# A three-MoE network: the branch for overfull experts moved behind the sixth pair, small loads issued in the mixers

## The chip, the cores and the metric

The kernel runs on one core of a Trainium2 chip. The metric is the device time of one execution in microseconds (us), lower is better. A core has five engines that run their own instruction streams and meet through semaphores: TensorE (PE: matmuls; its weight loads are shown as PEld), VectorE (DVE), ScalarE (ACT), GpSimd (POOL) and SyncE (SP, which here only issues DMAs). 16 DMA engines carry all transfers between the chip's memory (HBM) and the on-chip memory. "PEq", "SPq" and so on are the engines' sequencers: branches, register loads, semaphore instructions, DMA issues.

## The reference

x has T = 256 tokens of D = 1024. Three layers follow each other, each a mixer and a mixture of experts (MoE): first the "even" mixer, then the "odd" mixer, then a "second" mixer of another kind, and a norm at the end. Cut to the MoE, of which all three are alike:

```python
g_logits = xt @ w_group + b_group;  g_sel = argmax(g_logits)            # 4 groups
p_g = softmax(g_logits)[g_sel]
e_in = (xt @ w_expert + b_expert).reshape(N, 4, 8)[:, g_sel]            # 8 experts of the group
top_v, top_i = lax.top_k(e_in, 2)                                       # 2 experts for each token
gate = p_g * softmax(top_v)
y_e = (silu(xr @ w1[e]) * (xr @ w3[e])) @ w2[e]                         # for the rows xr of expert e, hidden size 512
out = segment_sum(y * gate)                                             # back to the tokens
x = x + gate2 * out                                                     # gate2 in the first two layers only
```

All is float32. The weights of the 32 experts of one MoE are 192 MB (w1, w3, w2 of 2 MB each, times 32), and every one of them is read once. The inputs are fixed, so that the number of tokens of each expert is, too; no expert has over 64 tokens in any of the three MoEs.

## The kernel before

**Tiles.** The tokens lie in two tiles of 128. An expert has room for CAP = 64 tokens, and two experts make a pair, so a MoE is a loop over NP = 16 pairs. For pair p: `up(p, "g")` and `up(p, "u")` multiply the pair's gathered tokens `xg` with w1 and w3 (32 matmuls each), `turn(p)` transposes the product `hh` on PE into `ht`, `down(p)` multiplies with w2. `parts`, at the end of `down`, takes the product out of PSUM: DVE multiplies with `ga` into `sg`, ACT rounds into `yh`, POOL puts the rest into `yl`. `combine(p, t)` scatters yh and yl back to token tile t by matmuls with the one-hot `pg`, and DVE adds to `x`. `gather(j)` collects the tokens of pairs 2j and 2j + 1 into `xg` from the high and low parts `hh`, `hl` of the normed tokens. The loop delays the combine: `combine(p - 1, 0)` stands between the two ups of pair p, `combine(p - 1, 1)` behind its turn. `gather(p // 2 + 1)` stands between up "u" and the turn of each odd pair p.

**Weights.** All large weights go through a ring of RING = 18 slots of 1 MB. A list (`plan`) fixes the order of the loads; `pump` (its DMA is line 193) issues the next of them on SP whenever a slot is free, at the place of the program where `done` or `release` frees one. A pair needs 12 loads. In a MoE two slots hold `hh` and `hl`, and one holds `hT`, the transposed tokens; hT's slot is released behind the branch.

**DMA lanes.** The DMAs of SP and ACT share eight completion semaphores ("lanes", DMAHW0 to DMAHW7 in the rows of the order below) in the program's order. A DMA is issued only when the one that is eight places ahead of it has landed.

**Small loads.** `router(l)` issues four DMAs on ACT (the router's weights `wr` and biases `br` of MoE l), `bias_load` one of 1 MB (`bias` from `bvec`, in rows of 1 KB) for the odd mixer, `second_setup` eleven (constants of the second mixer: k_rope, k_rot, k_vmask and others). All stand in pair 0: MoE0's `start` issues bias_load(1) and router(1), MoE1's router(2) and second_setup, and MoE2 loads the final norm's weights (512 KB) there.

**The branch.** `overflow` reads the largest rank (`ti`) into a register of every engine (line 1716) and branches on it (line 1717): where an expert has over 64 tokens, a loop over all experts recomputes what did not fit. With the inputs of this kernel that body never runs, and each engine jumps over it. The branch stands behind gather(0), ahead of pair 0. Behind it SP waits for the lanes that the body uses, all eight.

The order of work in the mixers comes from `weave`, which interleaves generators by estimated times; instructions are issued in the order in which the program records them. In the odd mixer `gate_coeffs(1, 2)` ends with two copies on ACT into `ga`; ACT's next work is a CAST (line 460) that splits weights and three copies into `pT` for the attention's matmuls.

Of the kernel before, what the change touches and what calls it, by code (L numbers as in the profile page):

```python
# [9 lines left out]
FT = mybir.dt.float32  # L10
# [3 lines left out]
AF = mybir.ActivationFunctionType  # L14
OP = mybir.AluOpType
# [10 lines left out]
NEG = -1e30  # L26
E = 32
CAP = 64
RING = 18
SLOT = 2048  # L30
SCRATCH = 2048
# [90 lines left out]
class Net:  # L122
# [746 lines left out]
    def even(self, coeffs):  # L869
        nc = self.nc  # L870
        with self.tc.tile_pool(name="even", bufs=1, reuse_waits="tile") as g:
# [49 lines left out]
            def stream():  # L921
                yield from self.slab_tm(512, s_qa)

                def use_att():
                    s = self.slot()
                    self.att, self.ob = s[:, :1024], s[:, 1024:]
                    self.flag("att", 0.7)

                def use_vb():
                    s = self.slot()  # L930
                    self.vb, self.gs = (s[:, 1024 * i:1024 * i + 1024].rearrange("p (t d) -> p t d", t=NT) for i in range(2))

                yield from self.mix(self.slab_tm(256, s_ka), 8, self.ev[0])
                self.want(use_att)
                self.want(use_vb)
                yield from self.mix(self.slab_fm(4, s_qb), 16, self.ev[1])
                self.outputs(4)
                self.outputs(4)
                self.gate_coeffs(0, 2)
                yield (1.8, 5.0)  # L940
                self.router(0)
                yield from self.mix(self.slab_tm(512, s_vb), 8, self.ev[2])
                yield from self.mix(self.slab_tm(512, s_rb), 8, self.ev[3])
                self.release(2)
# [33 lines left out]
    def odd(self, coeffs):  # L978
        nc, A, tc = self.nc, self.A, self.tc
        with tc.tile_pool(name="odd", bufs=1, reuse_waits="tile") as g:  # L980
# [77 lines left out]
            def stream():  # L1058
# [3 lines left out]
                self.outputs(8)  # L1062
                yield from self.mix(self.slab_tm(512, s_v(4)), 8, self.od[1])
                self.gate_coeffs(1, 2)
                yield (3.8, 0.3)
                yield from self.mix(self.slab_tm(512, s_qk(3)), 8, self.od[2])
                yield from self.mix(self.slab_tm(512, s_qk(1)), 8, self.od[3])
# [369 lines left out]
    def second(self, coeffs):  # L1437
        nc, tc = self.nc, self.tc
        with tc.tile_pool(name="sec", bufs=1, reuse_waits="tile") as g:
# [98 lines left out]
            def stream():  # L1538
# [3 lines left out]
                yield from t(h, KC, [[(f, 0, P, s_kraw(1)), (0, P, 152, s_vv(1, 0)), (1, P, 152, s_vv(1, 1))]])  # L1542
                self.outputs(4)
                self.outputs(4)
                yield from self.slab_fm(4, s_q)
                yield from self.slab_fm(4, s_f)
                yield from self.slab_fm(4, s_hq)
# [162 lines left out]
        for i in range(n):  # L1710
            self.mm(p[:, :476], self.ident, self.km, True, True)

    def overflow(self, g, l, hT, h, rk, wt, ti, w1, w3, w2, gate):
        nc, tc = self.nc, self.tc
        wd = self.dp.tile([E, P, NT], FT, name="wd", tag="wd")
        rv = nc.values_load(ti, min_val=0, max_val=T, skip_runtime_bounds_check_because="rank < T")
        with tc.If(rv >= CAP):
            wv = g.tile([P, NT, E], FT, name="wv")
            nc.vector.tensor_scalar(wv, rk, float(CAP), None, op0=OP.is_ge)
            nc.vector.tensor_mul(wv, wv, wt)  # L1720
            nc.scalar.dma_start(wd.rearrange("e p t -> p t e"), wv, allow_slow_non_contiguous=True)
            if gate:
                self.gate_coeffs(l, 5)
            for t in range(NT):
                for k0 in (0, 4):
                    p = self.psum().rearrange("d (k q) -> d k q", k=4)
# [4 lines left out]
                        self.affine(hT[:, k0 + k, P * t:P * t + P], p[:, k], k0 + k, "v")  # L1731
            with tc.For_i(0, E, 1) as e:
                wc = g.tile([P, NT], FT, name="wc")
                nc.scalar.dma_start(wc, wd[bass.ds(e, 1)].rearrange("e p t -> (e p) t"))
                ho = g.tile([P, 4, T], FT, name="ho", tag="yh")
                chunk = lambda tag: g.tile([P, 512], FT, name=tag)
                for hc in range(4):
                    pp = [self.psum((P, T)), self.psum((P, T))]
                    for j in range(2):
                        c0 = P * hc + 64 * j  # L1740
                        for p, w, tag in zip(pp, (w1, w3), ("hh", "ht")):
                            c = chunk(tag).rearrange("p (k n) -> p k n", k=KC)
                            nc.scalar.dma_start(c, w[bass.ds(e, 1)].rearrange("e (p k) n -> (e p) k n", k=KC)
                                                [:, :, c0:c0 + 64])
                            for k in range(KC):
                                self.mm(p[64 * j:64 * j + 64], c[:, k], hT[:, k], k == 0, k == KC - 1)
                    nc.scalar.activation(ho[:, hc], pp[0], AF.Silu)
                    nc.vector.tensor_mul(ho[:, hc], ho[:, hc], pp[1])
                for nq in range(8):
                    c = chunk(("hh", "ht")[nq % 2]).rearrange("p (k n) -> p k n", k=4)  # L1750
                    nc.scalar.dma_start(c, w2[bass.ds(e, 1)].rearrange("e (k p) n -> (e p) k n", p=P)
                                        [:, :, P * nq:P * nq + P])
                    for t in range(NT):
                        p = self.psum((P, P))
                        for hc in range(4):
                            self.mm(p, ho[:, hc, P * t:P * t + P], c[:, hc], hc == 0, hc == 3)
                        tmp = g.tile([P, 512], FT, name="sg", bufs=2)
                        nc.vector.tensor_scalar(tmp[:, :P], p, wc[:, t:t + 1], None, op0=OP.mult)
                        if gate:
                            nc.vector.tensor_mul(tmp[:, :P], tmp[:, :P], self.ga[:, P * nq:P * nq + P])  # L1760
                        xs = self.x[:, t, P * nq:P * nq + P]
                        nc.vector.tensor_add(xs, xs, tmp[:, :P])

    def moe(self, l, mods, start, coeffs, slots, fill=None):
        nc, tc = self.nc, self.tc
        _, w1, w3, w2, gate = self.moe_args(l)
        with tc.tile_pool(name="moe", bufs=1, reuse_waits="tile") as g:
            hT = self.hT
# [157 lines left out]
            gather(0)  # L1926
            if late is not None:
                late()
            self.pump()
            self.overflow(g, l, hT, (hh, hl), rk, wt, ti, w1, w3, w2, gate)  # L1930
            self.release()
            weighted(0)
            for p in range(NP):
                last = p == NP - 1
# [11 lines left out]
                    turn(p)  # L1946
                else:
                    up(p, "g")
                    if p:
                        combine(p - 1, 0)  # L1950
                    else:
                        gather_w(0)
                        start()
                        if l == 2:
                            nc.scalar.dma_start(fw, self.A["final_norm_2"].rearrange("(o n) -> o n", o=1)
                                                .to_broadcast([P, D]))
                    up(p, "u")
                    if p % 2:
                        gather(p // 2 + 1)
                        if p == NP - 3:  # L1960
                            self.release(2, reserve=min(2, slots))
                    gather_w(p + 1)
                    turn(p)
                    if p:
                        combine(p - 1, 1)
                if fill is not None:
                    fill(p)
                (down_last if last else down)(p)
                if p == NP - 2:
                    coeffs()  # L1970
            if l == 2:
# [26 lines left out]
def body(tc, A, out):  # L1998
    with ExitStack() as ctx:
# [7 lines left out]
        n.plan_moe(2)  # L2007

        n.reserve = 6
        n.even(lambda: n.norm_coeffs(0, 7, 3, 4))  # L2010
# [9 lines left out]
        n.moe(0, n.ev[6], start0, lambda: n.norm_coeffs(1, 6, 0, 1), 8,  # L2020
              lambda p: 4 <= p < 8 and n.bias_flip(n.bias1, n.bias1, p - 4))
        n.odd(lambda: n.norm_coeffs(1, 7, 3, 4))
        bp.close()
        n.rb.close()
        pb = ctx.enter_context(ExitStack())
        pre = pb.enter_context(tc.tile_pool(name="pre", bufs=1))
# [6 lines left out]
        n.moe(1, n.od[5], start1, lambda: n.norm_coeffs(1, 8), 14)  # L2033
        n.fb.close()
        n.second(lambda: n.norm_coeffs(1, 9))
        pb.close()
# [29 lines left out]
```

## Time and profile before

| | |
|---|---|
| median of 3 runs | 2110.97 us (2109.19 to 2112.38) |
| the profiled execution | 2108.36 us |
| its span, first to last instruction | 2106.3 us |
| PE busy | 1901.6 us, 90% of the span |
| DVE, ACT, POOL busy | 858.1, 427.5, 327.9 us |
| moved by the DMA engines | 725.35 MB, 344 GB/s over the span |
| mean granted clock of TensorE | 0.968 |

MoE0's first up starts at 231.4 us, MoE1's at 879.4 and MoE2's at 1645.9; MoE0's pairs end at about 705, MoE1's at about 1340, and MoE2 runs to the end. The span is what the trace covers; the 2 us around it belong to the time. "Granted clock" is the share of TensorE's full 2.4 GHz; its lower level is 0.5 (1.2 GHz). An idle of an engine is put down to what released it; "issue" means that the profile shows no releaser.

### The profile page before, as it was taken

How to read it: one execution, taken by the hardware profiler on the slowest of the kernel's cores; microseconds unless marked ns; L12 is line 12 of the kernel's file. 1: busy time of each engine (PE TensorE's matmuls, PEld its weight loads, DVE VectorE, ACT ScalarE, POOL GpSimd, SP SyncE). 2: the span in 40 equal slices, each digit the busy share in tenths (PEclk: the TensorE clock that was granted, in tenths of full speed). 3: DMA queues.
4: the chain of work that ended last, by engine and by line, in shares of the span. 5: the costliest groups of instructions: out<-in, count | busy, mean ns of one | idle time of the engine just before them, and what ended most of it. 6: DMA issues, size and time to landing. Idle time of an engine off the chain costs nothing. (4 is left out here: it accounts for less than half of the span.)

```text
span 2106.3 us, 24926 instructions
## 1 busy us (share of the span) xinstructions
PE 1901.6 (90%) x9930; PEld 1056.1 (50%) x9930; DVE 858.1 (41%) x1574; ACT 427.5 (20%) x778; POOL 327.9 (16%) x248
## 2 busy tenths in 40 slices
PE   6888799999999899899999999998899899999997
PEld 3656344444444667534444444586788344444443
DVE  3665333333322567533332232467666333232223
ACT  1423101111100343211110011254544111010011
POOL 1331100000000334100000000142444000000000
PEclk8998899999999999999999999998999999999999
DMA  9697799999999856799999999921357799999997
GB/s 323 238 319 297 260 422 421 422 421 421 421 421 406 300 222 244 294 365 421 421 421 421 421 421 421 326 101 41 125 194 300 292 421 421 421 421 422 421 421 285
DMA packets 157547, 725.35 MB, mean 344 GB/s; under 512 B 25305, under 2 KB 43088, under 8 KB 85226
## 3 DMA queue, kind: packets, MB, share of 16 engines
q1 hardware_dynamic: 139216, 716.84, 84.9%
q10 hardware_dynamic: 18201, 6.76, 1.3%
q8 instruction: 85, 1.39, 0.3%
q14 instruction: 45, 0.36, 0.0%
HBM read 722.48 MB, written 1.07 MB: 344 GB/s over the span
## 5 line engine op out<-in xcount | busy, mean ns | idle before, releaser
L257 PE MATMUL ps<-slot,xg 128*64 128x512 f32 x2992 | 710.5, 599 | 20.6 <-DMA slot<-moe_w 9.6
L257 PEld LDWEIGHTS ps<-slot,xg 128*64 128x64 f32 x2992 | 254.4, 138 | 422.0 <-issue 359.8
L257 PE MATMUL ps<-slot,ht 128*64 128x512 f32 (+1 forms) x1552 | 345.0, 574 | 56.4 <-issue 49.2
L257 PE MATMUL ps<-slot 128*128 128x256 f32 (+8 forms) x2230 | 368.4, 327 | 15.1 <-DVE slot L461 9.6
L257 PEld LDWEIGHTS ps<-slot 128*128 128x128 f32 (+3 forms) x2230 | 300.5, 187 | 73.6 <-issue 14.0
L257 PEld LDWEIGHTS ps<-slot,ht 128*64 128x64 f32 x1552 | 128.7, 139 | 228.4 <-issue 213.9
L1891 DVE TENSOR_TENSOR x<-x,ps 128x512 f32<-128x512 f32 x180 | 115.3, 682 | 277.0 <-PE ps L257 277.0
L1865 POOL TENSOR_TENSOR yl<-sg,yh 128x512 fp32r<-128x512 f32 (+1 forms) x68 | 82.5, 1213 | 884.8 <-ACT yh L1864 884.8
L462 POOL TENSOR_TENSOR slot<-slot 128x512 fp32r<-128x512 f32 (+2 forms) x108 | 164.4, 1539 | 273.2 <-ACT slot L460 261.9
L1844 DVE SCALAR_TENSOR_TENSOR hh<-sg,ws,ps 128x512 f32<-128x512 f32 x48 | 53.4, 1113 | 319.4 <-PE ps L257 179.8
L1864 ACT CAST yh<-sg 128x512 fp32r<-128x512 f32 (+1 forms) x68 | 40.3, 593 | 468.9 <-DVE sg L1863 468.9
L461 DVE TENSOR_TENSOR slot<-slot 128x512 fp32r<-128x512 f32 (+2 forms) x108 | 110.2, 1035 | 54.4 <-ACT slot L460 53.9
L1863 DVE TENSOR_TENSOR sg<-ps,ga 128x512 f32<-128x512 f32 (+1 forms) x68 | 44.9, 660 | 175.2 <-PE ps L257 175.2
L460 ACT CAST slot<-slot 128x1024 fp32r<-128x1024 f32 (+2 forms) x108 | 106.6, 1020 | 46.2 <-PE ps L257 27.3
L257 PEld LDWEIGHTS ps<-u,slot 128*128 128x128 f32 x768 | 96.9, 199 | 18.3 <-issue 17.0
L257 PE MATMUL ps<-u,slot 128*128 128x256 f32 x768 | 101.9, 293 | 0.0
L1840 ACT ACTIVATE sg<-ps 128x512 f32<-128x512 f32 x48 | 28.7, 598 | 312.4 <-PE ps L257 312.4
L257 PE MATMUL ps<-yh,pg 128*128 128x512 f32 (+1 forms) x204 | 87.1, 429 | 0.7 <-ACT yh L1864 0.7
L257 PE MATMUL ps<-yl,pg 128*128 128x512 f32 (+1 forms) x204 | 77.5, 382 | 0.9 <-POOL yl L1865 0.8
L1916 POOL TENSOR_TENSOR slot<-x,rows 128x512 f32<-128x512 f32 x2 | 2.5, 1272 | 464.5 <-DVE x L1912 464.5
L398 ACT ACTIVATE xg<-ps,cf 128x256 f32<-128x256 f32 x64 | 36.2, 565 | 156.6 <-PE ps L257 156.6
L1867 ACT CAST yh<-ps 128x512 fp32r<-128x512 f32 (+1 forms) x34 | 19.1, 561 | 227.3 <-PE ps L257 227.2
(334 smaller groups left out, 1586.4 us busy)
## 6 DMA issues: line engine op xcount, KB each, us to landing
slot<-moe_w SPq DMA_DIRECT2D x376, 1024.0 KB, 19.8
slot<-w_gate SPq DMA_DIRECT2D x59, 1024.0 KB, 17.7
slot<-w_up SPq DMA_DIRECT2D x59, 1024.0 KB, 19.8
slot<-w_down SPq DMA_DIRECT2D x50, 1024.0 KB, 18.1
slot<-ada_w SPq DMA_DIRECT2D x48, 1024.0 KB, 7.7
slot<-w_in SPq DMA_DIRECT2D x20, 1024.0 KB, 8.5
slot<-odd_w_in SPq DMA_DIRECT2D x12, 1024.0 KB, 13.1
more<-w_down SPq DMA_DIRECT2D x10, 1024.0 KB, 19.8
```

What stands on the lines that cost most here:

```text
L257: self.nc.tensor.matmul(out, lhsT=lhsT, rhs=rhs, start=start, stop=stop)
L398: self.nc.scalar.activation(out, p, AF.Identity, scale=a, bias=nb[:, k:k + 1])
L460: nc.scalar.copy(wh, src)
L461: nc.vector.tensor_sub(wl[:, 0], src[:, 0], wh[:, 0].bitcast(FT))
L462: nc.gpsimd.tensor_sub(wl[:, 1], src[:, 1], wh[:, 1].bitcast(FT))
L1840: nc.scalar.activation(sg, ps, AF.Silu)
L1844: nc.vector.scalar_tensor_tensor(ha.rearrange("s k p -> s p k"), st["sg", p].rearrange("s (p k) -> s p k", k=4), st["ws", p], ps.rearrange ...
L1863: nc.vector.tensor_mul(y, ps, self.ga[:, sl])
L1864: nc.scalar.copy(yh, y)
L1865: nc.gpsimd.tensor_sub(yl, y, yh.bitcast(FT))
L1867: nc.scalar.copy(yh, ps)
L1891: nc.vector.tensor_add(self.x[:, t, sl], self.x[:, t, sl], ps)
```

## The change

Four things are moved. (1) The branch stands behind `down` of pair LATE = 5, the sixth; ahead of it both combines of pair 5, behind it gather(3), which were a pair later and ahead of pair 5's turn. (2) The body is written anew, with three DMAs in a loop inside a loop, so that its DMAs use three lanes. (3) hT's slot is released as soon as the router's logits are there. (4) The small loads are issued in the mixers ahead: bias_load(1) in the even mixer, router(1) and second_setup in the odd one, router(2) and the final norm's weights in the second.

```diff
@@ even mixer
                 self.router(0)
+                self.bias_load(1, self.bias1)
@@ odd mixer
                 self.gate_coeffs(1, 2)
+                self.router(1)
+                self.second_setup(self.pre)
                 yield (3.8, 0.3)
@@ second mixer
                 self.outputs(4)
+                self.router(2)
...
                 coeffs()
+                nc.scalar.dma_start(self.rows[1], self.A["final_norm_2"].rearrange("(o n) -> o n", o=1).to_broadcast([P, D]))
@@ overflow
             with tc.For_i(0, E, 1) as e:
...
+                with tc.For_i(0, 4, 1) as c:
                     pp = [self.psum((P, T)), self.psum((P, T))]
+                    for p, w, tag in zip(pp, (w1, w3), ("yh", "yl")):
+                        wt_ = g.tile([P, KC, P], FT, name="w" + tag, tag=tag)
+                        nc.scalar.dma_start(wt_, w[bass.ds(e, 1)].rearrange("e (p k) n -> (e p) k n", k=KC)
+                                            [:, :, bass.ds(c * P, P)])
...
+                    wt_ = g.tile([P, D], FT, name="wd", tag="yh")
+                    nc.scalar.dma_start(wt_, w2[bass.ds(e, 1)].rearrange("e h n -> (e h) n")[bass.ds(c * P, P)])
@@ moe
             self.route_logits(1)
+            self.release()
...
-            self.pump()
-            self.overflow(g, l, hT, (hh, hl), rk, wt, ti, w1, w3, w2, gate)
-            self.release()
             weighted(0)
...
                     up(p, "g")
-                    if p:
+                    if p and p - 1 != LATE:
                         combine(p - 1, 0)
-                    else:
+                    elif not p:
                         gather_w(0)
                         start()
-                        if l == 2:
-                            nc.scalar.dma_start(fw, self.A["final_norm_2"].rearrange("(o n) -> o n", o=1)
-                                                .to_broadcast([P, D]))
                     up(p, "u")
-                    if p % 2:
+                    if p % 2 and p != LATE:
                         gather(p // 2 + 1)
...
                     turn(p)
-                    if p:
+                    if p and p - 1 != LATE:
                         combine(p - 1, 1)
...
                 (down_last if last else down)(p)
+                if p == LATE:
+                    combine(p, 0)
+                    combine(p, 1)
+                    self.overflow(g, l, (hh, hl), rk, wt, ti, w1, w3, w2, gate)
+                    gather(p // 2 + 1)
@@ body
-        def start0():
-            n.bias_load(1, n.bias1)
-            n.gate_coeffs(0, 5)
-            n.router(1)
...
-        def start1():
-            n.gate_coeffs(1, 5)
-            n.router(2)
-            n.second_setup(pre)
```

In the rows of the order below a row with x2 or more stands for so many alike; line numbers of helpers are higher by one in the changed kernel (L193 is L194, L257 is L258), those of the branch by five. The order on SP, MoE0, where the branch stood: the last load of the first ring, the rank's load into a register, the branch and its first inner jump, which names the lanes.

```order
L193 DMA slot<-moe_w 128x2048 [waits DMAHW0_49,PE_49]
L1716 TENSOR_LOAD ti [waits DVE_49]
L1717 COMPARE_AND_BRANCH
L1732 COMPARE_AND_BRANCH
L1732 UNCONDITIONAL_BRANCH [waits DMAHW0_49,DMAHW1_49,DMAHW2_49,DMAHW3_49,DMAHW4_49,DMAHW5_49,DMAHW6_49,DMAHW7_49]
```

And where it stands in the changed kernel, 73 rows further on, behind the loads that pairs 0 to 5 release.

```order
L194 DMA slot<-moe_w 128x2048 [waits DMAHW2_49,PE_49]
L1721 TENSOR_LOAD ti [waits DVE_49]
L1722 COMPARE_AND_BRANCH
L1737 COMPARE_AND_BRANCH
L1737 UNCONDITIONAL_BRANCH [waits DMAHW3_49,DMAHW4_49,DMAHW5_49]
```

SP's branch moved past the loads of six pairs, and the lanes that it names are three, the oldest ones, where there were eight.

The order on PE, MoE0, around the branch, first in the kernel before: the end of gather(0), the branch, the first rows of the body (the body has 234 rows of matmuls in all, counting repeats).

```order
L257 MATMUL ps<-u,slot 128x256 [waits PE_49]
L257 MATMUL ps<-u,slot 128x256 x7
L1716 TENSOR_LOAD ti [waits DVE_49]
L1717 COMPARE_AND_BRANCH
L257 MATMUL ps<-rows_121,sel 128x512 [waits DVE_49,PE_49]
L257 MATMUL ps<-rows_121,sel 128x512
```

Then in the changed kernel: the end of pair 5's down (ht), both halves of combine(5) (yh, yl), the branch. Its body has 67 rows.

```order
L258 MATMUL ps<-slot,ht 64x512 x6
L258 MATMUL ps<-yh,pg 128x512 [waits PE_49,Activation_49]
L258 MATMUL ps<-yl,pg 128x512 [waits Pool_49]
L258 MATMUL ps<-yh,pg 128x512 [waits PE_49,Activation_49]
L258 MATMUL ps<-yl,pg 128x512 [waits Pool_49]
L258 MATMUL ps<-yh,pg 128x512 [waits PE_49]
L258 MATMUL ps<-yl,pg 128x512
L258 MATMUL ps<-yh,pg 128x512
L258 MATMUL ps<-yl,pg 128x512
L1721 TENSOR_LOAD ti [waits DVE_49]
L1722 COMPARE_AND_BRANCH
```

The combine stands directly behind the down that it needs and waits for ACT and POOL; behind the body gather(3) follows, whose first matmul waits for DVE.

The order on ACT in the odd mixer, before: the two copies into ga, and behind them a CAST that splits weights and the copies into pT.

```order
L248 COPY slot<-ps 128x512 [waits PE_49,Pool_49]
L248 COPY ga<-ps 128x512 [waits PE_49] x2
L460 CAST slot<-slot 128x1024 [waits DMAHW0_49]
L248 COPY pT<-ps 128x384 [waits PE_49] x3
L253 CAST slot<-ps 128x256 [waits DMAHW5_49,PE_49]
```

In the changed kernel 15 DMA issues stand behind the two ga copies, the four of the router, k_rope, k_ropec and k_rot first; here are the last eight, and what follows them.

```order
L1135 DMA k_csel<-k_csel 30x128 [waits DMAHW3_49]
L1135 DMA k_vmask<-k_vmask 128x512 [waits DMAHW4_49]
L1135 DMA pos<-cmp_pos 16x128 [waits DMAHW5_49]
L1135 DMA k_cmp<-k_cmp 128x64 [waits DMAHW6_49]
L1135 DMA k_causal<-k_causal 128x256 [waits DMAHW7_49]
L1135 DMA k_scan<-k_scan 128x256 [waits DMAHW0_49]
L1135 DMA hn<-hg_norm 128x128 [waits DMAHW1_49]
L1135 DMA ll<-hg_lb_logits 8x128 [waits DMAHW2_49]
L461 CAST slot<-slot 128x1024
L249 COPY pT<-ps 128x384 [waits PE_49] x3
```

The CAST and the copies into pT moved behind 15 issues, each of which waits for a lane.

## Rows read from the trace of the kernel before

**Rows 1.** The page: PE's busy time; GB/s in 40 slices of the span.
```profile
PE 1901.6 (90%) x9930; PEld 1056.1 (50%) x9930; DVE 858.1 (41%) x1574; ACT 427.5 (20%) x778; POOL 327.9 (16%) x248
...
GB/s 323 238 319 297 260 422 421 422 421 421 421 421 406 300 222 244 294 365 421 421 421 421 421 421 421 326 101 41 125 194 300 292 421 421 421 421 422 421 421 285
```
**Rows 2.** Window of MoE0's middle: length, engines' busy us, PEclk, DMA share, GB/s.
```profile
core 0: us, PE busy (x) PEld busy (x) DVE busy (x) ACT busy (x) POOL busy (x), PEclk, DMA share, GB/s
300.00:480.00 180.00, 169.47 (x818) 72.90 (x816) 58.03 (x89) 18.95 (x32) 15.32 (x12) 1.00 1.01 421
```
**Rows 3.** PE's waits in MoE0 (two rows), MoE1, MoE2: total, times, longest.
```profile
PEld ps L257 <- DMA slot<-moe_w: 13.2, 12, 2.2
...
PE ps L267 <- DVE hh L1844: 8.4, 9, 1.3
...
PEld ps L257 <- DMA slot<-moe_w: 13.6, 11, 1.6
...
PEld ps L257 <- DMA slot<-w_up: 5.4, 8, 1.6
...
PEld ps L257 <- DMA slot<-w_gate: 1.8, 2, 1.5
```
**Rows 4.** Windows at the start of MoE0 and MoE1.
```profile
224.00:240.00 16.00, 11.85 (x51) 5.82 (x51) 3.75 (x7) 2.98 (x4) 0.00 (x0) 0.73 0.31 91
240.00:264.00 24.00, 20.79 (x94) 7.02 (x92) 6.70 (x12) 3.00 (x5) 2.22 (x2) 1.00 0.92 348
872.00:888.00 16.00, 12.05 (x64) 7.23 (x62) 5.92 (x17) 4.14 (x6) 0.00 (x0) 0.92 0.59 208
888.00:916.00 28.00, 25.97 (x116) 9.08 (x118) 7.46 (x12) 3.01 (x5) 2.54 (x2) 1.00 0.86 310
231.40:236.00 4.60, 4.57 (x12) 1.48 (x14) 0.00 (x0) 0.00 (x0) 0.00 (x0) 0.50 0.54 208
```
**Rows 5.** PE's first up in MoE0 (timeline); waits for L1717, MoE1 and MoE2.
```profile
231.44 2.83 PE L257 MATMUL ps<-slot,xg 128*64 128x512 f32 x6 [4.15 <-issue]
...
PE ps L257 <- DVEq L1717: 2.8, 1, 2.8
...
PE ps L257 <- DVEq L1717: 1.8, 1, 1.8
```
**Rows 6.** Waits of SP's DMA issues, 880 to 912, MoE1.
```profile
SPq L193 <- DMA br<-b_grp: 11.1, 1, 11.1
...
SPq L193 <- DMA k_vmask<-k_vmask: 6.9, 1, 6.9
```
**Rows 7.** Timelines of DVE, ACT, POOL behind a down of MoE0, second half.
```profile
401.73 0.69 DVE L1863 TENSOR_TENSOR sg<-ps,ga 128x512 f32<-128x512 f32 x1 [0.96 <-PE ps L257]
...
402.45 0.62 ACT L1864 CAST yh<-sg 128x512 fp32r<-128x512 f32 x1 [1.03 <-DVE sg L1863]
...
403.15 1.27 POOL L1865 TENSOR_TENSOR yl<-sg,yh 128x512 fp32r<-128x512 f32 x1 [0.37 <-ACT yh L1864]
```
**Rows 8.** Lines 1717 and 1716: ns min/median/max, first and last start in us.
```profile
L1717 PEldq COMPARE_BRANCH  x3: 3578/3798/3818, 224.9 to 1641.6; - x3
...
L1717 DVEq COMPARE_BRANCH  x3: 56/63/72, 228.6 to 1645.0; - x3
L1717 DVEq EVENT_SEMAPHORE  x3: 21/21/21, 229.8 to 1645.5; - x3
...
L1716 DVEq TENSOR_LOAD <-ti x3: 312/317/550, 227.9 to 1644.6; - x3
```
**Rows 9.** Timeline of ACT in MoE1's pair 0: first, third, last of 15 issues.
```profile
890.39 0.58 ACTq L1592 DMA_DIRECT2D wr<-w_grp  x1
...
891.80 3.72 ACTq L1594 DMA_DIRECT2D br<-b_grp  x1
...
901.48 0.34 ACTq L1131 DMA_DIRECT2D ll<-hg_lb_logits  x1
```
**Rows 10.** Timelines of ACT and PE in the odd mixer, the pT copies and matmuls.
```profile
767.26 1.24 ACT L248 COPY pT<-ps 128x384 f32<-128x384 f32 x3 [0.18 <-PE ps L267]
...
769.11 2.17 PE L257 MATMUL ps<-pT,slot 128*128 128x128 f32 x18
```

More of the change, by code (lines that the diff above doesn't have):

```diff
@@ L28 @@
 CAP = 64
+LATE = 5
 RING = 18
@@ L1711, in warm, with overflow @@
             self.mm(p[:, :476], self.ident, self.km, True, True)
-    def overflow(self, g, l, hT, h, rk, wt, ti, w1, w3, w2, gate):
+    def overflow(self, g, l, h, rk, wt, ti, w1, w3, w2, gate):
         nc, tc = self.nc, self.tc
-        wd = self.dp.tile([E, P, NT], FT, name="wd", tag="wd")
         rv = nc.values_load(ti, min_val=0, max_val=T, skip_runtime_bounds_check_because="rank < T")
@@ L1720, in overflow @@
             nc.vector.tensor_mul(wv, wv, wt)
-            nc.scalar.dma_start(wd.rearrange("e p t -> p t e"), wv, allow_slow_non_contiguous=True)
-            if gate:
-                self.gate_coeffs(l, 5)
+            cnt = g.tile([P, 1], FT, name="top")
+            nc.vector.memset(cnt, 0.0)
+            hT = g.tile([P, KC, T], FT, name="xg")
             for t in range(NT):
@@ L1733, in overflow @@
                 wc = g.tile([P, NT], FT, name="wc")
[L1734 to L1737, printed above, removed]
-                    pp = [self.psum((P, T)), self.psum((P, T))]
[L1739 to L1752, printed above, removed]
-                    for t in range(NT):
[L1754 to L1762, printed above, removed]
+                for t in range(NT):
+                    tmp = g.tile([P, 512], FT, name="sg", bufs=2)
+                    nc.vector.scalar_tensor_tensor(tmp[:, :E], self.iota[:, :E], cnt, wv[:, t],
+                                                   op0=OP.is_equal, op1=OP.mult)
+                    nc.vector.tensor_reduce(wc[:, t:t + 1], tmp[:, :E], axis=AX.X, op=OP.add)
@@ new lines, in overflow @@
+                nc.vector.tensor_scalar(cnt, cnt, 1.0, None, op0=OP.add)
+                with tc.For_i(0, 4, 1) as c:
+                    pp = [self.psum((P, T)), self.psum((P, T))]
+                    for p, w, tag in zip(pp, (w1, w3), ("yh", "yl")):
+                        wt_ = g.tile([P, KC, P], FT, name="w" + tag, tag=tag)
+                        nc.scalar.dma_start(wt_, w[bass.ds(e, 1)].rearrange("e (p k) n -> (e p) k n", k=KC)
+                                            [:, :, bass.ds(c * P, P)])
+                        for k in range(KC):
+                            self.mm(p, wt_[:, k], hT[:, k], k == 0, k == KC - 1)
+                    ho = g.tile([P, T], FT, name="ho", tag="uw")
+                    nc.scalar.activation(ho, pp[0], AF.Silu)
+                    nc.vector.tensor_mul(ho, ho, pp[1])
+                    wt_ = g.tile([P, D], FT, name="wd", tag="yh")
+                    nc.scalar.dma_start(wt_, w2[bass.ds(e, 1)].rearrange("e h n -> (e h) n")[bass.ds(c * P, P)])
+                    for t in range(NT):
+                        for n in range(2):
+                            sl = slice(512 * n, 512 * n + 512)
+                            p = self.psum()
+                            self.mm(p, ho[:, P * t:P * t + P], wt_[:, sl], True, True)
+                            tmp = g.tile([P, 512], FT, name="sg", bufs=2)
+                            nc.vector.tensor_scalar(tmp, p, wc[:, t:t + 1], None, op0=OP.mult)
+                            if gate:
+                                nc.vector.tensor_mul(tmp, tmp, self.ga[:, sl])
+                            xs = self.x[:, t, sl]
+                            nc.vector.tensor_add(xs, xs, tmp)
@@ L1767, in moe @@
         with tc.tile_pool(name="moe", bufs=1, reuse_waits="tile") as g:
-            hT = self.hT
             hh, hl = (self.slot(FR).rearrange("p (t k q) -> p t k q", t=NT, k=KC) for i in range(2))
@@ L2009, in body @@
         n.reserve = 6
-        n.even(lambda: n.norm_coeffs(0, 7, 3, 4))
         bp = ctx.enter_context(ExitStack())
         n.bias1 = bp.enter_context(tc.tile_pool(name="bias", bufs=1, side="right")).tile([P, 8, T], FT, name="bias1")
-        def start0():
-            n.bias_load(1, n.bias1)
-            n.gate_coeffs(0, 5)
-            n.router(1)
-        n.moe(0, n.ev[6], start0, lambda: n.norm_coeffs(1, 6, 0, 1), 8,
+        n.even(lambda: n.norm_coeffs(0, 7, 3, 4))
+        n.moe(0, n.ev[6], lambda: n.gate_coeffs(0, 5), lambda: n.norm_coeffs(1, 6, 0, 1), 8,
               lambda p: 4 <= p < 8 and n.bias_flip(n.bias1, n.bias1, p - 4))
+        pb = ctx.enter_context(ExitStack())
+        n.pre = pb.enter_context(tc.tile_pool(name="pre", bufs=1))
         n.odd(lambda: n.norm_coeffs(1, 7, 3, 4))
@@ L2024, in body @@
         n.rb.close()
-        pb = ctx.enter_context(ExitStack())
-        pre = pb.enter_context(tc.tile_pool(name="pre", bufs=1))
-        def start1():
-            n.gate_coeffs(1, 5)
-            n.router(2)
-            n.second_setup(pre)
-        n.moe(1, n.od[5], start1, lambda: n.norm_coeffs(1, 8), 14)
+        n.moe(1, n.od[5], lambda: n.gate_coeffs(1, 5), lambda: n.norm_coeffs(1, 8), 14)
         n.fb.close()
```

## The prediction

> **What bounds the kernel now.** I read the page first, then the stages one by one. The page gives PE 90% of the span, and its GB/s line says where the other limit lies: 421 in nearly every slice that belongs to a MoE, 41 to 365 in the mixers [rows 1]. The window of MoE0's middle shows both at once: DMA share 1.01, and PE busy for 169.47 of 180 us [rows 2]. So each MoE has two limits close together. At 421 GB/s a load of 1 MB (1,048,576 bytes) takes 2.49 us, twelve of them for a pair 29.9 us. PE's own work for a pair is less (169.47/180 × 29.9 = 28.2 at this window's pace), so PE eats the ring's lead and then waits for loads: 13.2 us in MoE0, 13.6 in MoE1, 5.4 + 1.8 in MoE2 [rows 3].
>
> The end of a MoE therefore comes from the DMA engines, and what counts is the time in which they did not run at 421. I read that at the start of the MoEs [rows 4]. In MoE0, 224 to 240 moved 91 GB/s (12.5 us lost of 16), and 240 to 264 moved 348 (24 × 73/421 = 4.2 us lost). In MoE1, 872 to 888 moved 208 (8.1 lost), and 888 to 916 moved 310 (28 × 111/421 = 7.4 lost). The first stretch of each is a full ring that waits for PE's first matmuls; the second is where the small loads stand.
>
> PE's first up matmuls come late because of the branch: 4.15, 2.8 and 1.8 us idle in the three MoEs [rows 5]; in MoE0 the clock then stands at 0.50 (the lower of its two levels) for 4.6 us, which costs 2.3 more [rows 4]. In the second stretch SP stands behind lanes that small ACT loads hold: 11.1 and 6.9 us in MoE1 [rows 6].
>
> **The change, MoE by MoE.** *DMA side.* PE starts 4.15 + 2.3 us earlier in MoE0 and frees the first slots that much earlier; with the small loads and the 1 MB bias gone, the 4.2 us of the second stretch come back too: 10.6. MoE1: 2.8 + 7.4 = 10.2. MoE2: 1.8, and the 512 KB of the final norm at 421 GB/s are 1.2: 3.0. The early release of hT's slot lets one load more go out while the ring is full; before, it went out in the same dead time, so I count 0 (upper bound one load, 2.5 each).
>
> *PE side, the branch after pair 5.* What PE pays there, from a pair of MoE0: combine(5) follows its own down instead of standing a pair later. Behind the end of down come DVE 0.69, ACT 0.62, POOL 1.27 for the second half [rows 7], so the last yl is ready at 404.42, 2.7 us after down's end (about 401.7). combine(5,0)'s first matmuls fill part of that, and I count 1.9 idle. Pair 5 loses gather(3) between up and turn, which covered the wait for hh; turns without one show 0.9 there (8.4 us in 9 waits for hh) [rows 3]. Then the branch: PE's next wait needs DVE past it, as in before, where PE waited for DVE's L1717 [rows 5]. DVE adds the last combine to x, loads the rank (0.32 to 0.55), branches (0.06) and posts its semaphore 0.5 to 1.2 us later (228.6 to 229.8 in MoE0, 1645.0 to 1645.5 in MoE2) [rows 8]: with 0.7 for the add, 1.6 to 2.6, I take 2.3. Sum 5.1, and 1 for the clock, which may fall after it as it did in MoE0 (2.3 at about two in five): 6 per MoE. Bounds: 4, and 5.1 + 2.3 + 4 = 11 if the whole branch gap of MoE0 returns.
>
> PE's own branch took 3.58 to 3.82 us, against 0.06 to 0.07 on DVE [rows 8]. PE jumped over 234 rows of matmuls in before, DVE over 79; PE's body has 67 now. If PE keeps its 3.8, it starts about when the last yl is there and ends 4 us later, a gap of some 2.8 instead of 2.3; if it falls to DVE's, nothing of it is seen. I take the 2.3, and the difference is at most 1.5 in three MoEs. The Trainium skill ("Runtime: NRT & Kernel Launch", section "Instruction fetch mechanics") says that a taken branch to a target outside the window already fetched stalls until the target's page has come. This trace agrees as far as it goes (3.8 us for the long jump, 0.06 for short ones). By that rule the shorter body would make PE's branch cheap, and the sum would be the one that I take.
>
> PE's account is then: MoE0 13.2 + 4.15 + 2.3 − 6 = 13.6 us to gain before PE itself is the limit, MoE1 13.6 + 2.8 − 6 = 10.4, MoE2 7.2 + 1.8 − 6 = 3.0. The smaller of the two accounts is the gain: 10.6, 10.2, 3.0, in sum 23.8. Where both meet (MoE1, MoE2) neither is reached in full, so I take 22. Bounds 15 (6 us per MoE become 9) and 30 (hT's slot counts, the branch costs 4).
>
> SP's stop at the branch now waits for three lanes, not eight. With eight loads on the way, five remain while it stands, 12.4 us of transfer. I count 0.
>
> *The odd mixer.* ACT gets 15 issues in a row behind the two ga copies. In MoE1 the same 15 took from 890.39 to 901.82, 11.4 us, of which 3.72 in one that waited for a lane [rows 9]. In the mixer the lanes are freer, so I take 9.0 (that one at about 1.3). Behind them stand a CAST and the pT copies, at 767.26 now [rows 10]; PE's pT matmuls start at 769.11, and the first copy (0.41) is ready at 767.67, so 1.4 are covered. PE stalls 9.0 − 1.4 = 7.6 us, and after such a stop the clock falls as at 231.4, another 2.3: 10. Bounds: 4, if PE's later waits for DVE give half back, and 15, if the 11.4 return and SP, which issues no load until the last lanes are free, makes PE wait for weights.
>
> *The other two mixers.* The bias of 1 MB stands in front of even_w_in: 0 to 2.5 us of DMA time, I take 1, since only part of it falls where the engines idle. In the second mixer the four router issues stand before ACT's next work; three of them took 5.1 us in MoE1 [rows 9], mostly lane wait. I take 1.5 (0 to 5). The Trainium skill ("DMA: Bandwidth & Descriptors", section "Issuing engines are not separate DMA queues") speaks against a gain from such moves: whichever engine issues, the same 16 engines carry it, and only issue time is saved. By that alone the bias would cost its 2.5 us in full in the even mixer, 1.5 us over my sum; no row here shows that stretch with it.
>
> **Sum.** −22 + 10 + 1 + 1.5 = −9.5. The profiled execution took 2108.4, so 2098.9 there. It lies 2.6 below the median 2110.97 of the runs; on the median it is **2101.5**.
>
> **Rivals.**
> - *The odd mixer hides the block.* PE waits there for DVE anyway now and then, and DVE runs on while ACT issues. Against it: the pT matmuls have only 1.4 us of cover. Cost 2 instead of 10: 2093.5, at the best of the gains 2088.
> - *The odd mixer is dearer* (SP held as well): 17 to 20 instead of 10, so 2108 to 2111, no change. For it: SP's next load needs a lane of the last small ones, as it did in MoE1 for 18 us. Against: slots come free no faster while PE stands.
> - *SP's stop drains the DMA engines in mid-MoE.* If all loads had landed, a restart costs some 2.5 us, one load: 7.5 in three MoEs, 2109, no change. For it: DMA is the limit just then. Against: five loads are left.
> - *PE becomes the limit (the other side).* Place: the pause after down(5). With a pause of X us per MoE, PE's accounts are 19.6 − X, 16.4 − X and 9.0 − X, 45 − 3X in sum; against 12.5 of costs the kernel is over 0.2% slower when 45 − 3X is below 8.3, from X = 12.2 on. At X = 13 it is 2110.97 + 12.5 − 6 = 2117.5. For it: my upper bound is 11, and gather, turn and clock follow each other there. Against: the same branch gave 4.15 at most in before.
>
> **How the numbers follow.** Forecast 0.57, odd mixer hidden 0.15, odd mixer dearer 0.10, SP drained 0.09, PE the limit 0.09. 0.2% is 4.2 us here, about what a measurement can tell from no change. Faster by more takes nearly all of the forecast and the first rival and a little of the next two: 0.76. Same 0.15, slower 0.09. The range goes from the best of the hidden case, cut at 2091, to the dear cases at 2110; below lies about 0.06, above 0.13. The forecast's own range is 2094 to 2107.
>
> **What the next profile would show.** Right: no idle before up(0) of over 1 us; the GB/s line at 421 from some 20 us into MoE0 and MoE1 on; SP's longest waits are for PE, not for small loads; an idle of about 5 us on PE after down(5), and the waits for moe_w grown or unchanged; a hole of 7 to 10 us on PE before the odd mixer's pT matmuls. Wrong: a lower clock for long behind pair 5, PE never waiting for moe_w again (then PE is the limit), a dip of the GB/s in pair 6, or no hole in the odd mixer.

## The result, and the profile after

The changed kernel takes 2088.4 us (median of 4 runs, 2084.29 to 2090.57), the kernel before 2110.08 beside it: ratio 0.9898, 95% interval 0.9874 to 0.9922, so 21.7 us or 1.0% faster (17 to 27). Forecast were 9.5 us and a range of 2091 to 2110: the sign was right, the size less than half, and the median lies below the range.

The profiled execution took 2084.29, the fastest of the four and 4.1 under their median; its span is 2082.1 (before: 2106.3). The page, PE and GB/s by slice, against [rows 1]:

```profile
PE 1878.9 (90%) x9930; PEld 1034.6 (50%) x9930; DVE 857.0 (41%) x1574; ACT 427.6 (21%) x778; POOL 327.9 (16%) x248
...
GB/s 321 240 307 302 331 422 421 421 421 421 421 421 406 329 193 258 303 404 421 421 420 421 421 421 421 316 99 55 129 200 311 307 421 421 420 421 421 421 421 283
```

The same number of matmuls cost PE 22.7 us less, and the slice ahead of the first one at 421 rose from 260 to 331 in MoE0 and from 365 to 404 in MoE1. Where the time went, by stage (the even mixer counts from the span's start; a MoE counts from the end of gather(0) to the end of its last down, so that its start is in it; the first column is the mean of two profiles of the kernel before, the second taken later as e8):

| stage | before | after | change | forecast |
|---|---|---|---|---|
| even mixer | 228.0 | 230.4 | +2.5 | +1 |
| MoE0 | 470.8 | 455.0 | −15.9 | −10.6 |
| odd mixer | 178.2 | 184.2 | +6.0 | +10 |
| MoE1 | 468.7 | 457.5 | −11.2 | −10.2 |
| second mixer | 298.9 | 296.0 | −2.9 | +1.5 |
| MoE2 | 452.0 | 448.5 | −3.5 | −3.0 |

The changes add up to 25.0, over 3 more than the medians differ by, and one profile of a stage is not sure to some 4 us: in e5 and e9, whose MoE0 is the same program as the changed kernel's, it took 457.6 and 459.6. A firmer mark is the end of pair 13's down, before the last pairs run at one clock or the other: from the end of gather(0) it came at 409.6 and 410.0 in the two profiles of before, and at 395.9 in the changed kernel.

The windows at the start of MoE0 and MoE1 after, laid about the first up as there (it starts 6.4 and 7.5 us into the two pairs of windows; 7.4 in both before), against [rows 4]:

```profile
224.00:240.00 16.00, 14.58 (x70) 8.73 (x69) 6.85 (x22) 4.36 (x8) 0.00 (x0) 0.85 0.47 186
240.00:264.00 24.00, 22.30 (x103) 7.48 (x103) 5.98 (x8) 2.41 (x4) 2.55 (x2) 1.00 1.00 399
862.00:878.00 16.00, 15.00 (x71) 8.00 (x70) 8.30 (x28) 4.44 (x8) 0.00 (x0) 0.84 0.65 250
878.00:906.00 28.00, 25.89 (x107) 8.70 (x108) 6.34 (x10) 2.48 (x5) 2.55 (x2) 0.94 0.97 389
```

The second stretches now move 399 and 389 GB/s, where 348 and 310 stood; what is lost there is 1.3 and 2.1 us, not 4.2 and 7.4. GB/s counts every byte, though, the small loads' own too. The bytes by queue in MoE0's second stretch (240 to 264: packets, MB, share; q1 carries SP's loads, q10 ACT's), before and after:

```profile
q1 hardware_dynamic: 976, 7.11, 72.7%
q10 hardware_dynamic: 3408, 1.21, 19.1%
```

```profile
q1 hardware_dynamic: 1312, 9.57, 99.6%
```

So the weights gained 2.46 MB there, 5.8 us at 421 GB/s. In MoE1's second stretch they went from 7.50 to 10.86 MB, 8.0 us.

The timeline of PE at MoE0's start has the first up right behind gather(0) at the full clock (the 4.15 of [rows 5] gone), and SP's waits in MoE1's first pairs are for PE alone, against [rows 6]:

```profile
224.39 6.04 PE L258 MATMUL ps<-u,slot 128*128 128x256 f32 x32
230.36 1.94 PE L258 MATMUL ps<-slot,xg 128*64 128x512 f32 x8
```

```profile
SPq L194 <- PE ps L258: 42.0, 8, 15.4
```

PE's waits for loads, against [rows 3]: MoE0 (two rows), MoE1, MoE2.

```profile
PEld ps L258 <- DMA slot<-moe_w: 3.6, 8, 1.5
...
PE ps L268 <- DVE hh L1850: 9.4, 10, 1.3
...
PEld ps L258 <- DMA slot<-moe_w: 2.8, 9, 0.5
...
PEld ps L258 <- DMA slot<-w_up: 2.9, 5, 1.6
```

13.2, 13.6 and 7.2 us are down to about 3 each: the two limits of a MoE now meet. The tenth wait for hh is pair 5's turn without its gather.

The pause behind pair 5, PE's timeline in MoE0 from the first matmul of combine(5):

```profile
395.49 0.51 PE L258 MATMUL ps<-yh,pg 128*128 128x512 f32 x1
396.70 0.50 PE L258 MATMUL ps<-yl,pg 128*128 128x512 f32 x1 [0.71 <-POOL yl L1871]
397.05 0.47 PE L258 MATMUL ps<-yh,pg 128*128 128x512 f32 x1
398.38 0.50 PE L258 MATMUL ps<-yl,pg 128*128 128x512 f32 x1 [0.86 <-POOL yl L1871]
...
401.12 4.00 PE L258 MATMUL ps<-u,slot 128*128 128x256 f32 x32 [1.32 <-DVEq L1722]
```

0.71 and 0.86 are the wait for yl (forecast 1.9), 1.32 the wait for DVE past its branch (forecast 2.3). Over the whole of MoE0 PE's account grew by 2.4 in the combines, 1.4 in the gathers, 1.2 in the turns: 5.0, forecast 5.1. The clock did not fall, and 395 to 410 moved 418 GB/s: SP's stop for three lanes cost nothing. The branch itself, against [rows 8]:

```profile
L1722 PEldq COMPARE_BRANCH  x3: 329/334/444, 399.0 to 1787.2; - x3
...
L1722 DVEq COMPARE_BRANCH  x3: 62/63/72, 400.5 to 1788.6; - x3
L1722 DVEq EVENT_SEMAPHORE  x3: 21/21/21, 401.1 to 1789.2; - x3
```

PE's jump over the short body takes 0.33 us, where 3.58 to 3.82 stood.

The odd mixer, ACT's first and last issue of the 15 and what follows, then PE, against [rows 9, 10]:

```profile
750.42 0.57 ACTq L1598 DMA_DIRECT2D wr<-moe_w_group  x1
...
758.11 0.53 ACTq L1135 DMA_DIRECT2D ll<-hg_lb_logits  x1
758.68 1.04 ACT L461 CAST slot<-slot 128x1024 fp32r<-128x1024 f32 x1 [7.67 <-DMA k_causal<-k_causal]
759.63 1.23 ACT L249 COPY pT<-ps 128x384 f32<-128x384 f32 x3
```

```profile
760.15 4.21 PE L258 MATMUL ps<-pT,slot 128*128 128x128 f32 x18 [6.03 <-ACT pT L249]
```

The 15 issues took 8.2 us (750.42 to 758.64; forecast 9.0), PE stood 6.03 (7.6), and the pT matmuls behind it ran 4.21 instead of 2.17 at the lower clock (forecast 2.3).

### The profile page after: what moved, and what is told of

Same layout as the page of the kernel before. It is cut to its first block, busy times and chain, and to the rows that moved or that the text cites. A ratio compares the mean times of both kernels' runs of the same rounds, so it can differ in the third digit from the quotient of the medians.

```text
span 2082.1 us, 24910 instructions
## 1 busy us (share of the span) xinstructions
PE 1878.9 (90%) x9930; PEld 1034.6 (50%) x9930; DVE 857.0 (41%) x1574; ACT 427.6 (21%) x778; POOL 327.9 (16%) x248
## 5 line engine op out<-in xcount | busy, mean ns | idle before, releaser
L258 PE MATMUL ps<-slot,xg 128*64 128x512 f32 x2992 | 686.1, 595 | 1.4 <-DMA slot<-w_up 0.7
L258 PEld LDWEIGHTS ps<-slot,xg 128*64 128x64 f32 x2992 | 237.1, 137 | 392.2 <-issue 365.5
L258 PE MATMUL ps<-slot,ht 128*64 128x512 f32 (+1 forms) x1552 | 345.0, 574 | 54.3 <-issue 46.2
L258 PE MATMUL ps<-slot 128*128 128x256 f32 (+8 forms) x2230 | 366.2, 325 | 18.5 <-DVE slot L462 9.3
L258 PEld LDWEIGHTS ps<-slot 128*128 128x128 f32 (+3 forms) x2230 | 298.6, 185 | 76.7 <-issue 14.9
L258 PEld LDWEIGHTS ps<-slot,ht 128*64 128x64 f32 x1552 | 127.1, 138 | 227.4 <-issue 208.8
L258 PEld LDWEIGHTS ps<-u,slot 128*128 128x128 f32 x768 | 96.7, 198 | 21.2 <-issue 15.0
L258 PE MATMUL ps<-u,slot 128*128 128x256 f32 x768 | 101.7, 292 | 3.9 <-DVEq L1722 3.5
L258 PE MATMUL ps<-yh,pg 128*128 128x512 f32 (+1 forms) x204 | 87.2, 429 | 0.8 <-ACT yh L1870 0.7
L258 PE MATMUL ps<-yl,pg 128*128 128x512 f32 (+1 forms) x204 | 78.2, 386 | 4.3 <-POOL yl L1871 4.0
L399 ACT ACTIVATE xg<-ps,cf 128x256 f32<-128x256 f32 x64 | 36.1, 564 | 140.6 <-PE ps L258 140.6
```

Source lines behind the costliest of these rows:

```text
L258: self.nc.tensor.matmul(out, lhsT=lhsT, rhs=rhs, start=start, stop=stop)
L399: self.nc.scalar.activation(out, p, AF.Identity, scale=a, bias=nb[:, k:k + 1])
```

## The experiments

Each was run beside the kernel before, which had medians of 2107.0 to 2109.5 in the three batches.

| run | median us | ratio to before (95%) |
|---|---|---|
| changed kernel | 2088.4 | 0.9898 (0.9874 to 0.9922) |
| e1_branch_only | 2093.6 | 0.9929 (0.9903 to 0.9954) |
| e2_loads_only | 2103.4 | 0.9972 (0.9954 to 0.9990) |
| e3_ht_late | 2089.1 | 0.9914 (0.9885 to 0.9942) |
| e4_long_body | 2102.1 | 0.9966 (0.9953 to 0.9979) |
| e5_odd_on_sp | 2084.7 | 0.9887 (0.9862 to 0.9911) |
| e6_short_body_old_place | 2096.5 | 0.9937 (0.9912 to 0.9961) |
| e7_old_place_odd_on_sp | 2088.2 | 0.9899 (0.9872 to 0.9927) |
| e9_all_on_sp | 2090.6 | 0.9916 (0.9892 to 0.9941) |
| e10_branch_after_pair_nine | 2087.8 | 0.9896 (0.9867 to 0.9925) |
| e8_before_again, e11_body_mid | 2109.2, 2100.9 | one run each |

**e1: the branch's part alone.** All small loads back in pair 0.

```diff
-                self.bias_load(1, self.bias1)
-                self.router(1)
-                self.second_setup(self.pre)
-                self.router(2)
...
+        def start0():
+            n.bias_load(1, n.bias1)
+            n.gate_coeffs(0, 5)
+            n.router(1)
```

> The changed kernel with all small loads back in pair 0 (bias, routers, constants, final norm), the branch still behind pair 5 and hT's slot released early. Theory A (each part adds up as the windows of before say): the second stretch of MoE0 loses 4.2 us again, that of MoE1 7.4, MoE2 1.2, while the even mixer gives back 3.1 and the odd mixer 7.7: 12.8 - 10.8, about 2090 us against 2088.4 of the changed kernel, and no hole ahead of the odd mixer's pT matmuls. Rival B (the small loads in pair 0 were also what cost MoE0 the surplus of 7 us that the forecast missed, through the ring's lead): 2095 to 2100.

2093.6: between the two. By stage against the changed kernel, MoE0 lost 9.2, MoE1 7.1, MoE2 nothing, and the odd mixer gave back 7.1. In MoE0 1.7 of it was there from pair 0's down on (the clock was 0.94 over 30 us, as in e5 without these loads; 1.00 in the changed kernel), and 7.5 by pair 13's down: 5.8 us of loads, as many as the bytes above say, where the window of before had shown 4.2. The last 1.7 came in the last pair, at 0.95.

**e2: the loads' part alone**, the kernel before with the loads in the mixers.

```diff
+                self.bias_load(1, self.bias1)
+                self.router(1)
+                self.second_setup(self.pre)
+                self.router(2)
...
-            n.bias_load(1, n.bias1)
-            n.router(1)
-            n.second_setup(pre)
```

> The kernel before with only the small loads moved into the mixers; branch, body and hT's slot as before. Theory A: MoE0 gains 4.2, MoE1 7.4, MoE2 1.2, mixers cost 10.8: about 2 us less than before, no change by 0.2 per cent. Rival B: the moved loads are worth 7 us more in MoE0: 9 us less than before. In both, PE's idle of 4.15, 2.8 and 1.8 us ahead of the first ups stays.

6.0 us less, between the theories. 15.8 for e1 and 6.0 for e2 make 21.8: on the medians the two parts add up to the whole. By the intervals e1 is worth 10 to 20 us and e2 2 to 10. Beside the old branch the loads gave MoE0 5.0 to 5.1 us from its first up to pair 13's down (3.7 to 4.1 from the end of gather(0), since e2's first up came later).

**e3: hT's slot released at the old place.**

```diff
             self.route_logits(1)
-            self.release()
...
                 late()
+            self.release()
             weighted(0)
```

> The changed kernel with hT's slot released ahead of pair 0, where before released it, and not behind the router's logits. Theory A (the slot is worth one load, 2.5 us, of DMA time in MoE0 and in MoE1, and less in MoE2): the ring holds 15 loads and not 16 at the first up, and the time is 4 to 6 us longer, about 2093. Rival B (the load only moves inside dead time): 2088, the same lead a pair later.

2089.1, and MoE0 and MoE1 within 0.2 us in the profiles: rival B. The early release is worth nothing that could be seen, as the prediction had counted it.

**e4 and e11: a longer body that never runs.**

```diff
                 nc.vector.tensor_scalar(cnt, cnt, 1.0, None, op0=OP.add)
+                self.warm(170)
```

(60 in e11.)

> The changed kernel with 170 further matmuls in the branch's body, which is never run, so that PE jumps over 237 rows of matmuls as in before (234), not 67. Theory A (the length of the jump sets the price): PE's branch takes 3.5 to 3.9 us in place of 0.33, its idle ahead of gather(3) grows from 1.3 to about 3 us, and the time grows by 0 to 3 us, since PE waits for loads later anyway. Rival B (the place sets it): 0.33 us still, and 2088.

> The changed kernel with 60 further matmuls in the body that never runs, so that PE jumps over 127 rows of matmuls, between 67 (0.33 us) and 237 (6.07 us). Theory A (there is a length up to which the jump is cheap, and it lies above this): 0.33 us. Rival B (it lies below): 5 to 6 us and some 10 us more in all. If the price grows with the length: about 2.4 us.

e4 took 2102.1, 13.7 more than the changed kernel. PE's branch, of e4 and then of e11:

```profile
L1722 PEldq COMPARE_BRANCH  x3: 6058/6073/6141, 401.9 to 1804.0; - x3
```

```profile
L1722 PEldq COMPARE_BRANCH  x3: 5977/6033/6181, 401.0 to 1800.1; - x3
```

127 rows cost what 237 do, and 67 cost 0.33: a step between 67 and 127, no price by length. Theory A of e4 holds for the cause and fails for the size; in e11 rival B holds. PE's timeline in e4, where 1.32 stood, and the window behind it:

```profile
408.17 4.18 PE L258 MATMUL ps<-u,slot 128*128 128x256 f32 x18 [5.41 <-PEq L1722]
```

```profile
408.00:415.00 7.00, 6.16 (x32) 5.98 (x32) 1.14 (x3) 1.70 (x3) 0.00 (x0) 0.65 1.02 421
```

4.1 us more idle, and the clock falls behind it: by pair 6's down e4's MoE0 is 7.1 us late, and by pair 13's still 5.5 (e11: 6.3 and 4.6). That is the prediction's last rival at work, PE as the limit, from a pause of about 12 us (5.0 + 7.1); but the kernel stayed 7.4 us faster than before, where that rival's sum gives 3.5 slower at 12.

**e5: the odd mixer's 15 loads on SP.**

```diff
-                self.router(1)
-                self.second_setup(self.pre)
+                self.router(1, nc.sync)
+                self.second_setup(self.pre, nc.sync)
```

> The changed kernel with the 15 loads of the odd mixer issued by SP at the same place, not by ACT. Theory A (the price there is ACT's issue time ahead of the pT copies): PE's stop of 6 us ahead of the pT matmuls and the low clock behind it go, 7 to 8 us less than the changed kernel: about 2081. Rival B (SP, held for the same 9 us, brings the weights late instead): PE waits for weights in the odd mixer or at MoE1's start, 2088.

2084.7, 3.7 less. The hole is gone; PE's timeline at the pT matmuls:

```profile
758.50 1.63 PE L258 MATMUL ps<-slot 128*128 128x512 f32 x6
759.97 2.17 PE L258 MATMUL ps<-pT,slot 128*128 128x128 f32 x18
```

The odd mixer took 179.9 (changed kernel 184.2), in e7 176.5, as long as before. Theory A for the mechanism, and half of its 7 us on the median (2.3 by the ratios, since the kernel before was faster in e5's batch); the intervals of e5 and the changed kernel overlap.

**e6, e7: the short body at the old place**, with hT kept in its slot for it; e7 with e5's edit too.

```diff
                 late()
+            self.pump()
+            self.overflow(g, l, hT, (hh, hl), rk, wt, ti, w1, w3, w2, gate)
+            self.release()
             weighted(0)
...
-                if p == LATE:
-                    combine(p, 0)
-                    combine(p, 1)
-                    self.overflow(g, l, (hh, hl), rk, wt, ti, w1, w3, w2, gate)
-                    gather(p // 2 + 1)
```

> The changed kernel with the branch back behind gather(0), ahead of pair 0, but with the new short body (hT kept in its slot for it, released behind the branch). Theory A (the body's length was the price, not the place): PE's branch takes under 0.5 us, the first ups start 1 to 2 us after gather(0), the 5.1 us per MoE behind pair 5 go, and since the loads are nearly the limit the time is 2083 to 2089. Rival B (the place matters, since the DMA engines stand still there): the starts cost 4 us each as before, 2094 or more.

> Both edits, the short body at the old place and the odd mixer's loads on SP: theory A of both gives the sum of the two differences, 2076 to 2082; if either rival holds, no better than the better of the two runs.

e6 took 2096.5, 8.1 more than the changed kernel: rival B. PE's jump is 0.34 us there, and yet the first up waits:

```profile
235.15 1.08 PE L258 MATMUL ps<-slot,xg 128*64 128x512 f32 x4 [2.63 <-DVEq L1722]
```

It is DVE's place past the branch that PE waits for, 2.63, 2.63 and 1.30 us in the three MoEs. The 5 us pause is absent, and by pair 13's down e6 stands in MoE0 where the changed kernel does (389.1 and 388.9 us from the first up): the pause behind pair 5 is free, the one ahead of pair 0 is not. e6 differs from e2 in the body alone, and from the changed kernel in the place (and hT's slot, worth nothing in e3): on the medians the shorter body with its three lanes gave 7.0 us at the old place, and the new place 8.1 more, though the intervals of e2 and e6 just overlap. e7 gained 8.2 on e6, so the loads on SP help there in full; but at 2088.2 it is no better than e5, and the 2076 to 2082 of its theory A fell.

**e8: the kernel before once more.**

> The kernel before once more, for a second profile. Theory A (the 3.3 us that the second mixer seemed to gain, and the 3.1 that the even mixer seemed to lose, are the granted clock and the start of that one execution): its second mixer takes about 296 us, not 299.3, and its even mixer 227 to 236. Rival B (they are the moved loads): 299 and 227 again. MoE0 and MoE1 within 3 us of the first profile.

Theory A for the even mixer only in part (228.7), and rival B for the second mixer (298.6 beside 299.3). MoE0 took 464.2 us from its first up, not 468.6, so outside the 3 us named. A pair of windows at MoE0's end, of before and of e8, shows the difference to be the granted clock:

```profile
664.00:676.00 12.00, 12.00 (x40) 6.44 (x42) 2.35 (x6) 0.62 (x1) 2.32 (x2) 0.72 1.01 412
```

```profile
661.00:673.00 12.00, 12.00 (x54) 6.49 (x50) 1.79 (x5) 1.24 (x2) 2.56 (x2) 1.00 1.01 420
```

40 matmuls in 12 us at 0.72, 54 at 1.00. One profile's stage can be 4 us off for that alone.

**e9 and e10: more on SP, and the branch later**, both on top of e5.

```diff
+                self.router(0, nc.sync)
+                self.bias_load(1, self.bias1, nc.sync)
+                self.router(2, nc.sync)
```

```diff
-LATE = 5
+LATE = 9
```

> The kernel of the run with the odd mixer's loads on SP (2084.7 us), and also router(0), the bias and router(2) issued by SP. Theory A (what the loads cost in the even and second mixers is ACT's issue time): 1 to 3 us less, about 2082.5. Rival B (ACT had room there, and SP's weights now wait behind the bias): no change or up to 3 us more.

> The kernel of the run with the odd mixer's loads on SP (2084.7 us), and the branch behind pair 9, the tenth, not the sixth. Theory A (the 5.1 us pause on PE costs nothing wherever loads come back as the limit behind it): 2083 to 2087, PE's waits for loads in pairs 9 to 13 fall by what the pause gives the ring. Rival B (later, there are fewer pairs left to win the pause back, and SP's wait for three lanes falls where the loads are the limit): 2 us more in each MoE, 2088 to 2092.

e9 took 2090.6, 6.0 more than e5; theory A falls, and so does B's bound of 3: its profile has the even mixer at 235.6, the second at 298.5 and MoE1 at 458.9, all above e5, which doesn't settle how much of it is the bias ahead of the weights. e10 took 2087.8, between the two theories, with runs from 2080.5 to 2089.0, too wide to tell from e5. PE's waits for loads fell in MoE0 (2.9 to 1.7 us) and grew in MoE1 (1.0 to 2.7), so theory A's sign doesn't show either.

## Why the prediction was wrong

**What held.** The order of limits (loads first, PE close behind), the gap ahead of pair 0, the small loads behind SP's waits, the pause of 5 us that costs nothing, no drained DMA engines, nothing from hT's slot, the hole in the odd mixer with its low clock. No rival came true: the time fell at the edge of what "the odd mixer hides the block" had put (2088 at best, or 2101.5 − 8 − 8 = 2085.5 by its own terms; the range stopped at 2091), but the hole is there. SP was held too, 30.1 us behind k_csel, as the second rival has it, yet no wait of PE for weights shows behind it. One sign was wrong: PE's waits for moe_w did not grow or stay, they fell to about 3, which is what the prediction's own two accounts leave for MoE0 (13.6 − 10.6).

**The step that failed is the sum**, in several terms, all but the even mixer's off the same way; the first is a misreading, the others sizes.
- *MoE0's 10.6.* Measured 15.9 against the mean of two profiles, 13.8 of it by pair 13's down. The second stretch was priced by its GB/s, as if all of the 348 were weights; 1.21 MB were the bias and the router's own bytes, 2.9 us at 421. So 4.2 + 2.9, less the 1.3 that stay lost, make the 5.8 of the queues and of e1. (For MoE2 the final norm's bytes were counted; in MoE1 the same slip leaves out 2.8, and 2.1 stay lost.) The rest is clock, as far as it shows: e5, the same MoE0 with a stretch at the lower clock at its start, gained 12.5 by pair 13's down, and in the profile on which the sum stood, MoE0's last pair ran partly at the lower clock (0.72 over 12 us) and took 36.1 us, against 31.9 in e8 and in the changed kernel.
- *"Neither is reached in full, so I take 22."* They were: MoE1 gave 11.2 for 10.2, MoE2 3.5 for 3.0. In MoE2 the parts don't add up: e1 and e2 give 3.7 and 3.3 there, and both together 3.5. That needn't be the smaller of two accounts: its last pair took 30.0 and 29.9 us at the full clock in e1 and e2, and 31.7 at 0.95 in the changed kernel.
- *The odd mixer's 10.* The stage grew by 6.0, the pT matmuls alone by 8.0 (6.0 of idle and 2.0 of lower clock): 8.2 us of issues stood for the 9.0, and 6.0 for the 7.6.
- *The second mixer's +1.5.* It took 2.9 less. It took 295.3 to 296.3 us in every run but before, e8 and e9, also in e1, where it holds no moved load. In e1, e2 and the changed kernel the same matmuls ran shorter there: the granted clock over 240 us of the stage was 0.93 in both profiles of before, 0.94 in e1 and 0.95 in the changed kernel. Why is open. The one cost of the moved loads that shows is a wait of 1.67 us ahead of a matmul with k_rot.
- *The even mixer's +1* came as a wait of 2.7 us ahead of one matmul behind the bias, where before, e8 and e1 show 0.8 to 1.3 (4.2 in e2 and e9, 2.7 to 3.2 in the others); the rest is no more than what this stage differs by between kernels (231.6 in e1, without the bias).

By parts: the loads were forecast at −12.8 + 12.5, nothing, and gave 6.0, outside its interval; the branch at 11.1 (4.15 + 2.3 + 2.8 + 1.8), and gave 15.8, with 11.1 inside the interval. Taking 22 for 23.8 was the other 1.8. So the loads' part is the one that is shown to be mis-sized.

**PE's own branch** I had weighed at 1.5 us at most in the sum. That term was mis-sized nearly tenfold: had the jump stayed long, it would have cost 13.7 (e4). The forecast was not hurt, since it took the short one. The Trainium skill ("Runtime: NRT & Kernel Launch", section "Instruction fetch mechanics") has the rule by which it was taken, that a target outside the fetched window makes the engine wait for its page; a step between 67 and 127 rows and the flat 6.0 us fit it. Where in between the step lies no run shows.

## What to carry to other kernels

A branch whose body is never run costs each engine its jump, and on PE here that hung on whether the body was short enough, not on how long it was: shorten it first, then put it where another limit hides the pause. Where two limits lie close, price a change on each and take the smaller, and don't shave that again. Price a stretch by the bytes of the loads that count, not by all GB/s: what small loads cost the weights is their waits and their own bytes. Small loads are dear where shared completion lanes stop the weights behind them, and as a block of issues on an engine that the next matmuls wait for: a queue that nobody waits for there is their place. In the odd mixer that was SP (e5, e7); moving the rest to SP as well took 6.0 us back (e9).

## What the hardware showed

- PE's jump over a long body took 3.58 to 3.82 us at the start of the MoEs, where the DMA engines moved 91 GB/s in MoE0's window and 208 in MoE1's (234 rows), and 6.0 to 6.2 in the middle of a MoE at 421 (237 and 127 rows). The profile's page lists a DMA queue for instructions; the Trainium skill, in the same section, says that the sequencer fetches through a DMA queue of its own, which fits a jump that is dearer under traffic. That traffic is the cause was not tried by itself.
- After a branch, a wait on another engine's semaphore was met only once that engine was past the branch itself, though the result that PE needed lay ahead of the branch: PE waited 1.1 to 1.3 us for DVE so in the changed kernel, where DVE had written gather(3)'s `u` 30 us earlier, and some 1.4 of the 2.63 in e6, where the last `xg` was written at 233.70 and PE began at 235.15. PE's own jump was 0.33 to 0.45 in both.
- The clock fell at each pause of 5.2 to 5.4 us on PE at the branch (e4 and e11, six of six), and at some of 1.0 to 1.3: in none of the changed kernel's three, but in MoE1 of e1, e5 and e9 and in two of e10's (0.66 over the 7 us behind it in e5), five of eighteen in the runs with the short body behind pair 5 or 9. So the same pause kept the clock or lost it, where the prediction had two in five.
- The last pair of MoE0 took 31.9 us at the full clock and up to 36.4 at 0.86 (e10), of the same matmuls; before and e8, the same kernel, took 36.1 and 31.9.
